# The up stage of a ConvFFN, last column: prompts copied out of their bank, a product moved whole, two moves at the front

## The chip, the core and the metric

The kernel runs on one core of a Trainium2 chip. The metric is the device time of one execution in microseconds (us), as the median of several runs.

A core has five engines, each with its own queue of instructions: TensorE (PE, the matmuls; PEld are its weight loads), VectorE (DVE), ScalarE (ACT), GpSimd (POOL) and SyncE (SP, which only issues transfers). They read and write the on-chip memory SBUF; matmuls write into PSUM, which has banks of 512 numbers of 32 bits in each of 128 partitions, and DVE and ACT read those. An engine waits on semaphores that another engine raises.

## The reference

One layer of a diffusion backbone for 1024 latent tokens (a grid of 16 rows of 64) and 128 context tokens ("prompts"), width 1024, everything in 32-bit floats. After a mixer comes the part that the change is in:

```python
def dw_conv(u, conv_w, conv_b, grid):   # grid: 3x3 depthwise; context: width 3
    ...
def conv_ffn(h, w_up, conv_w, conv_b, w_down, grid):
    u = dw_conv(h @ w_up, conv_w, conv_b, grid)
    gate, up = jnp.split(u, 2, axis=-1)
    return (jax.nn.silu(gate) * up) @ w_down
...
    x = x + gate2 * conv_ffn(h, w_ffn_up, ffn_conv, b_ffn_conv, w_ffn_down, grid)
```

The hidden width is 2 x 2816: `h @ w_up` has 5632 channels, half of them gates.

## The kernel before

**Precision.** A 32-bit product is made of three matmuls of a split: each operand x is a high part (`wuh`, `b11h`, ... copied with rounding by ACT, L1759 or L133) and a low part, x minus the high part (`wul`, `b11l`, ... one subtraction on POOL or DVE in `split_lo`, L69). So every product is (high, high), (high, low), (low, high) over four pieces of the contraction, 12 matmuls of 128x512.

**Up stage.** It makes `h @ w_up` for the grid's tokens in 22 columns c = 0 to 21 of 128 hidden channels, each with gates and ups. A column is done by a scheme of the Strassen kind with seven products (`up(c, p)`, L1976, L1777): 1 takes b11, 2 b21, 3 b22, 4 t4, 5 t1, 6 t2, 7 t3, where b and t are halves of the activations and their sums. They go into two accumulators of two banks each, `F = u[c][0]` (gates) and `S = u[c][1]` (ups); half of `S`, called X in the code, collects products 1, 6, 7 and 4. ACT copies X after product 1 (`cp`, by the name `p1`) and after product 6 (`u2p`, by the name `u2`), L1971, and DVE adds these copies to the others (L2134, L2135, L2160; in column 0 L1864, L1869, L1870 in `first_sums`). Product 6 cannot write X until `cp` has been copied, nor product 7 until `u2p` has. There are three accumulators for two that each column needs, so S of a column takes the banks of F of the column before, and F those of S two columns before.

**Convolution.** ACT writes the middle tap and the bias into `acc` (L1931), and DVE adds the eight other taps, each one `scalar_tensor_tensor` over the column (L1943, `acc <- u * weight + acc`, u in PSUM). The F convolution of a column runs before the S convolution (the second one, `second_half`). The last tap frees the accumulator. Then ACT takes the silu of the gates (L2043) and POOL multiplies gates by ups (L2045) and stores the result (L2046).

**Prompts.** The prompts of a column are 24 small matmuls (L2009); ACT copies them, PE transposes them (L2026) into a bank `x`, and `conv_prompt` does the width-3 convolution from there: one ACT instruction (L1956) and two DVE taps of 128x127 (L1960) for gates and the same for ups.

**Order.** PE's products go in the order of the loop at L2059: 5, (transposes and product 4 of the column before), 2, 3, 1, first prompt half, 6, second prompt half, 7. The last column differs: product 3 stands as six matmuls before product 1 and six behind, the prompts' halves go around product 7, and its product 4 has no next column to stand in. A scheduler orders the other engines' instructions by its own estimate of times, so a small edit can move rows far from it. POOL and DVE make the weights' low parts, POOL and SP issue the transfers.

**Down stage.** It begins behind the last column with product `xb` (L2279, 12 matmuls for each of 11 pairs of weights, `wuh`/`wul` or `wh`/`wl`), which goes into four banks; it takes the first three pairs through one bank after the other, then each further pair through all four. The third bank is that of the last column's transposed prompts. POOL makes the low parts of its first weight pairs, DVE those of pairs 7 to 10.

Of the kernel before, what the change touches and what calls it, by code (L numbers as in the profile page):

```python
# [12 lines left out]
AF = mybir.ActivationFunctionType  # L13
ALU = mybir.AluOpType
# [3 lines left out]
P = 128  # L18
# [6 lines left out]
NHID = 22  # L25
# [24 lines left out]
def kernel(ctx: ExitStack, tc: tile.TileContext, ins, outs, stop=None):  # L50
    nc = tc.nc
# [10 lines left out]
    anchor = {}  # L62
# [339 lines left out]
    for i in range(2):  # L402
# [3 lines left out]
        for v in range(2):  # L406
            dst = bass.AP(t.tensor, t.offset + v * pitch, [[32 * pitch, 2], [1, 512]])
# [4 lines left out]
    for i in range(2):  # L412
        ps = (ps_a, ps_mm)[i].tile([2 * 32, 512], F32, name="ada", tag=("ada", "mm")[i])
        psA.append(ps)
        for kt in range(KT):
# [4 lines left out]
            for j in range(2):  # L420
# [4 lines left out]
                    start=(kt == 0),  # L425
                    stop=(kt == KT - 1),
# [867 lines left out]
    def run(eng, fn):  # L1294

        if ran.get("free"):
            return fn()
        with tc.issue_after(ran[eng].ins) if eng in ran else nullcontext():
            ran[eng] = fn()
# [103 lines left out]
    tt = nc.vector.tensor_tensor  # L1403
# [7 lines left out]
    def half_hi(nm, n, raw):  # L1411
        run("act", lambda: nc.scalar.activation(HB["h"][nm][:, :, pieces[n]], raw, AF.Copy))
# [348 lines left out]
    def split_slots(c, names, eng):  # L1761
        hi, lo = split_parts(c, names)
        hi()
        return lo(eng)
# [5 lines left out]
        eng.tensor_tensor(r["s4"], r["12"], r["s2"], op=ALU.subtract)  # L1770
        return eng.tensor_tensor(r["s3"], r["11"], r["21"], op=ALU.subtract)

    def up_product(dst, c, a, b, start, stop, kts=range(4)):
        n = 3 * kts[0]
        for kt in kts:
            for x, y in (("h", "h"), ("h", "l"), ("l", "h")):
                last = mm(  # L1777
                    dst,
                    w_slot(c, a, x)[:, kt, :],
                    HB[y][b][:, kt, :],  # L1780
                    start=(start and n == 0),
                    stop=(stop and n == 11),
                    skip_group_check=True,
                )
                n += 1
        return last
# [71 lines left out]
    def first_sums():  # L1858

        F, S = u[0]  # L1860
        for n in range(2):
            token_sum(tmp[2 + n], rb(1, 0, n), tmp[2 + n])
        new_tiles("t4", 1)
        run("dve", lambda: tt(S[:, 512:NS], S[:, 0:512], copies["p5"], op=ALU.add))  # L1864
        half_hi("t4", 0, tmp[2])
        half_hi("t4", 1, tmp[3])
        for n in range(2):
            half_lo("t4", n, tmp[2 + n])
        run("dve", lambda: tt(F[:, 0:512], F[:, 0:512], copies["p1"], op=ALU.add))  # L1869
        run("dve", lambda: tt(F[:, 512:NS], F[:, 512:NS], copies["u2"], op=ALU.add))  # L1870
        second_lo("11", "12", eng="dve")

# [93 lines left out]
    def chained(fn):  # L1966

        run("pe", fn)
# [4 lines left out]
            return run("act", fn)  # L1973
        anchor["copy"] = fn()

    def up(c, p, kts=range(4)):  # L1976

        if p in (2, 3, 5):
            Z, Y = u[c][0][:, 0:512], u[c][0][:, 512:NS]
        else:  # L1980
            X = u[c][1][:, 0:512]
        chained(
            {
                1: lambda: up_product(X, c, "11", "b11", True, False),
                2: lambda: up_product(Z, c, "12", "b21", True, True),
                3: lambda: up_product(Y, c, "s4", "b22", False, True, kts),
                4: lambda: up_product(X, c, "22", "t4", False, True),
                5: lambda: up_product(Y, c, "s1", "t1", True, False),
                6: lambda: up_product(X, c, "s2", "t2", False, False),
                7: lambda: up_product(X, c, "s3", "t3", False, False),  # L1990
            }[p]
        )
        if p == 5 and c:
            copy(c, "p5", Y)
        elif p == 1:
            copy(c, "p1", X)
        elif p == 6:
            copy(c, "u2", X)
# [22 lines left out]
    def prompt_columns(c):  # L2021
        pp = ps_p.tile([P, 2, P], F32, name="x", tag="x")

        def turned():
            for i in range(2):
                last = nc.tensor.transpose(pp[:, i, :], pt_t[:, i * P : (i + 1) * P], ident)  # L2026
            return last

        chained(turned)
        up_first = SLOT[c]["21"] < SLOT[c]["11"]  # L2030
        with after("conv") if c < 2 else nullcontext():
            conv_prompt(pp[:, 1 if up_first else 0, :], c, acc[c][0])
            conv_prompt(pp[:, 0 if up_first else 1, :], 22 + c, acc[c][1])
# [25 lines left out]
    for c in range(NHID + 1):  # L2059
        n = c + 1 if c + 1 < NHID else None  # L2060
        if c < NHID:
            acc[c] = conv_tiles(c)
            u[c] = [ps_u.tile([P, NS], F32, name="u", tag="u")]

        if c == 0:
            u[0].append(ps_u.tile([P, NS], F32, name="u", tag="u"))
            for p in (1, 2):
                up(0, p)
        if c < NHID:
            up(c, 5)  # L2070
        if c == 0:
            prompt_work()
        if c == 1:
            for names in (("s2", "s4"), ("21", "22")):
                second_hi(*names)
                second_lo(*names)
            second_weights()
        if c == NHID:
            up(c - 1, 4)
            prompt_columns(c - 1)  # L2080
            second_half(c - 1)
        elif c > 0:
            prompt_columns(c - 1)
            up(c - 1, 4)
            second_half(c - 1)
        if c == NHID:
            break
        if c > 1 and n:
            split_slots(n, ("21", "22"), nc.gpsimd)
            if n + 1 < NHID:  # L2090
                load_row(n + 1, 2)
        last_c = c == NHID - 1
        if c > 0:
            up(c, 2)
            if not last_c:
                up(c, 3)
        pks[c] = ps_p.tile([P, 2 * P], F32, name="x", tag="x")
        if c == 1:
            up_prompt(c, 0)
            up_prompt(c, 1)  # L2100
        if c > 0:
            if last_c:
                up(c, 3, range(2))
            u[c].append(ps_u.tile([P, NS], F32, name="u", tag="u"))
            up(c, 1)
            if c == 1:
                anchor["p1"] = anchor["copy"]
                second_gate(0)
            if last_c:
                up(c, 3, range(2, 4))  # L2110
        if 1 < c and not last_c:
            up_prompt(c, 0)
        up(c, 6)
        if last_c:
            up_prompt(c, 0)
            up(c, 7)
        if c == 0:
            up(c, 3)
            up_prompt(c, 0)
            second_hi("s1")  # L2120
            second_lo("s1", eng="dve")
            second_hi("11", "12")
        if c and n:
            with tc.issue_after(anchor["p1"].ins) if c == 1 else nullcontext():
                split_slots(n, ("s1",), nc.gpsimd)
                split_slots(n, ("11", "12"), nc.gpsimd)
            if n + 1 < NHID:
                load_row(n + 1, 1)
        F, S = u[c]
        if c == 0:  # L2130
            up(c, 7)
            first_sums()
        else:
            nc.vector.tensor_tensor(F[:, 0:512], F[:, 0:512], copies["p1"], op=ALU.add)  # L2134
            nc.vector.tensor_tensor(F[:, 512:NS], F[:, 512:NS], copies["u2"], op=ALU.add)  # L2135
        if c != 1:
            up_prompt(c, 1)
        if c == 0:
            late = again["late"].tile([P, 2304], F32, name="late", tag="mh7")
            ss_t = late[:, 0:2048].rearrange("p (i n) -> p i n", i=4)  # L2140
            pt_t = late[:, 2048:2304]
        copy_pt = lambda: nc.scalar.activation(pt_t, pks[c], AF.Copy)
        if c == 0:
            run("act", copy_pt)
            with tc.issue_after(ran["act"].ins), tc.issue_after(ran["dve"].ins):
                anchor["conv"] = conv_rows(F, c, acc[c][0])
            ran["act"] = anchor["rows"]
        else:
            copy_pt()
        if c > 0 and n:  # L2150
            with tc.issue_after(anchor["copy"].ins) if c == 1 else nullcontext():
                split_slots(n, ("s2", "s4"), nc.gpsimd)
        if c == 1:
            with tc.issue_after(anchor["copy"].ins):
                split_slots(n, ("21", "22"), nc.gpsimd)
            load_row(n + 1, 2)
        if c > 0:
            if not last_c:
                up(c, 7)
            nc.vector.tensor_tensor(S[:, 512:NS], S[:, 0:512], copies["p5"], op=ALU.add)  # L2160
        if c > 0:
            anchor["conv"] = conv_rows(F, c, acc[c][0])
        if c > 0 and n:
            split_slots(n, ("s3",), nc.gpsimd)
            if n + 1 < NHID:
                weight_sums(n + 1, nc.gpsimd)
# [265 lines left out]
```

## Time and profile before

| | |
|---|---|
| runs | 1519.69, 1519.78, 1520.42 us; median 1519.78 |
| the profiled execution | 1517.37 us, its span 1515.2 us, mean granted clock of TensorE 0.996 |
| busy | PE 97%, DVE 76%, ACT 52%, POOL 47% of the span |
| PE's waits over 0.2 us from 785 us on, until the down stage has started | 785.18 (0.27), 797.88 (1.20), 801.58 (0.69), 806.01 (1.41), 809.49 (0.47), 834.18 (2.28), 1249.81 (1.28), 1271.72 (2.07) |

A row of a timeline reads: start in us, duration in us, engine, line of the kernel, operation, out<-in, shape, and how many instructions are joined in it (x2: the duration is that of both). In brackets is the time that the engine sat idle before it, and what it waited for. A row of the waits has the total in us, how many times, and the longest. A row of one line's instructions has min/median/max in ns. Column 1 of the up stage begins near 787 us, column 3 near 834; the last ends near 1265.

### The profile page before, as it was taken

The numbers are of one execution on the slowest core, as the hardware profiler recorded it, in microseconds if no ns is written. First come the engines' busy times: TensorE is split into PE (matmuls) and PEld (weight loads), VectorE is DVE, ScalarE is ACT, GpSimd is POOL, SyncE is SP. The second block draws the span as 40 slices with busy tenths as digits, with TensorE's granted clock in tenths as the row PEclk, the third lists the DMA queues.
The fourth block names the chain that finished last, engine by engine and source line by source line (L and its number), as shares of the span: only waits on it lengthen the run. The fifth ranks groups of instructions, "written<-read, shape, count | busy, mean of one in ns | idle before, by whom it ended". The sixth has DMA issues, their size and how long they took to land.

```text
span 1515.2 us, 31139 instructions
## 1 busy us (share of the span) xinstructions
PE 1464.7 (97%) x12509; PEld 1247.6 (82%) x12509; DVE 1145.1 (76%) x1735; ACT 781.1 (52%) x1519; POOL 705.0 (47%) x537
## 2 busy tenths in 40 slices
PE   6999999999999999899998999999999999999998
PEld 2898998999898988777776888888888877888886
DVE  3766566565565767755699999999999999689575
ACT  3575667555455455613765444444444444466444
POOL 1602122334333241222229999999999996100001
PEclk9999999999999999999999999999999999999999
DMA  9311111335535463967642745445644567989762
GB/s 341 134 44 48 45 57 52 117 98 171 162 97 184 120 203 121 334 247 251 219 142 89 244 115 144 119 119 139 196 119 139 169 154 215 371 267 368 241 191 115
DMA packets 173802, 253.79 MB, mean 167 GB/s; under 512 B 11828, under 2 KB 113698, under 8 KB 171738
## 3 DMA queue, kind: packets, MB, share of 16 engines
q1 hardware_dynamic: 150455, 173.52, 36.0%
q0 software_dynamic: 22592, 77.60, 16.6%
q8 instruction: 98, 1.61, 0.5%
q10 hardware_dynamic: 611, 0.68, 0.1%
q14 instruction: 46, 0.38, 0.1%
HBM read 191.93 MB, written 82.90 MB: 181 GB/s over the span
## 4 chain that ended last, share of the span: by engine, by line
PE 79%; DVE 7%; DMA 5%; ACT 3%; issue 3%; POOL 2%; SPq 0%; POOLq 0%; DVEq 0%; ACTq 0%
PE u L1777 24%; PE mm L625 15%; PE xb L2279 8%; PE yb L2279 6%; PE mm L639 5%; PE x L2009 4%; PE lv L964 3%; DVE acc L1943 3%; PE mm L777 2%; PE yb L2333 2%; PE u L1544 2%; PE x L1032 1%; PE mm L519 1%; DMA raw<-in_w_in_dram 1%; PE ada L1201 1%
## 5 line engine op out<-in xcount | busy, mean ns | idle before, releaser
L1943 DVE SCALAR_TENSOR_TENSOR acc<-u,convc,acc 128x945 f32<-128x945 f32 (+2 forms) x352 | 426.9, 1218 | 8.9 <-ACT acc L1931 1.8
L69 POOL TENSOR_TENSOR wl<-raw,wh 128x1024 fp32r<-128x1024 f32 x42 | 103.0, 2466 | 249.8 <-ACT wh L133 194.2
L625 PE MATMUL mm<-h1h,wh 128*128 128x384 f32 x528 | 185.0, 350 | 1.3 <-ACT qj L528 1.3
L625 PE MATMUL mm<-h1l,wh 128*128 128x384 f32 x528 | 179.0, 339 | 0.0
L625 PE MATMUL mm<-h1h,wl 128*128 128x384 f32 x528 | 179.0, 339 | 0.0
L927 DVE TENSOR_TENSOR Q<-Q,fb 128x384 f32<-128x384 f32 x126 | 81.9, 650 | 82.4 <-PE lv L964 81.4
L69 POOL TENSOR_TENSOR wul<-sr,wuh 128x512 fp32r<-128x512 f32 (+1 forms) x64 | 115.0, 1799 | 38.6 <-ACT wuh L1759 38.6
L69 POOL TENSOR_TENSOR wul<-ra,wuh 128x1024 fp32r<-128x1024 f32 x43 | 110.0, 2559 | 6.6 <-ACT wuh L133 6.5
L917 ACT ACTIVATE m<-k 128x384 f32<-128x384 f32 x126 | 70.2, 557 | 79.9 <-DVE k L929 37.2
L2243 POOL TENSOR_TENSOR sq<-sq,mhalf 128x1 f32<-128x1 f32 x9 | 11.1, 1231 | 205.8 <-DVE sq L2242 205.8
L625 PEld LDWEIGHTS mm<-h1h,wh 128*128 128x128 f32 x528 | 99.5, 188 | 6.2 <-issue 3.9
L625 PEld LDWEIGHTS mm<-h1l,wh 128*128 128x128 f32 x528 | 99.5, 188 | 0.6 <-issue 0.2
L625 PEld LDWEIGHTS mm<-h1h,wl 128*128 128x128 f32 x528 | 99.3, 188 | 0.8 <-issue 0.5
L639 PE MATMUL mm<-wh,h1h 128*128 128x256 f32 x288 | 83.8, 291 | 1.5 <-ACT v L664 1.5
L929 DVE TENSOR_TENSOR k<-k,fb 128x384 f32<-128x384 f32 x126 | 74.2, 589 | 12.3 <-ACT m L917 7.2
L639 PE MATMUL mm<-wh,h1l 128*128 128x256 f32 x288 | 80.4, 279 | 0.0
L639 PE MATMUL mm<-wl,h1h 128*128 128x256 f32 x288 | 80.4, 279 | 0.0
L133 ACT ACTIVATE wh<-raw 128x1024 fp32r<-128x1024 f32 x50 | 52.8, 1058 | 38.5 <-PE mm L625 11.6
L1971 ACT ACTIVATE u2p<-u 128x512 f32<-128x512 f32 x44 | 26.5, 602 | 77.3 <-PE u L1777 76.7
L1759 ACT ACTIVATE wuh<-ra 128x1024 fp32r<-128x1024 f32 x42 | 44.3, 1054 | 36.6 <-issue 22.1
L2045 POOL TENSOR_TENSOR acc<-acc,acc 128x1152 f32<-128x1152 f32 x22 | 60.0, 2730 | 5.0 <-DVE acc L1943 5.0
L1759 ACT ACTIVATE wuh<-sr 128x512 fp32r<-128x512 f32 (+1 forms) x63 | 48.7, 773 | 23.1 <-PE x L2009 16.4
(385 smaller groups left out, 4464.1 us busy)
## 6 DMA issues: line engine op xcount, KB each, us to landing
ra<-in_w_ffn_up_dram SPq DMA_DIRECT2D x84, 256.0 KB, 3.5
raw<-in_w_in_dram SPq DMA_DIRECT2D x32, 512.0 KB, 4.5
v<-in_w_ada_dram SPq DMA_DIRECT2D x27, 512.0 KB, 5.1
scr_g<-acc POOLq DMA_DIRECT2D x22, 576.0 KB, 5.6
scr_s<-late POOLq DMA_DIRECT2D x11, 1024.0 KB, 4.3
scr_t<-in_w_ffn_down_dram POOLq DMA_DIRECT2D x16, 704.0 KB, 7.3
wa<-in_w_ada_dram SPq DMA_DIRECT2D x16, 512.0 KB, 5.3
scr_t<-in_w_ffn_down_dram POOLq DMA_DIRECT2D x2, 2816.0 KB, 12.5
```

Of the source, the lines that this page charges most:

```text
L69: return eng.tensor_tensor(out, full, hi.bitcast(F32), op=ALU.subtract)
L625: anchor["fill"] = mm(ps, a[:, kt, :], h[kt][b], start=(n == 0), stop=(n == 23))
L639: anchor["fill"] = mm(ps, h[kt][t // 3][:, ts_], a[:, kt % 4, :], start=(n == 0), stop=(n == 23))
L917: nc.scalar.activation(aps(t, 0, [[2 * h, NB], [h, 2], [1, h]]), aps(src, 0, [[2 * h, NB], [BL + h, 2], [1, h]]), AF.Copy)
L927: nc.vector.tensor_tensor(qm, qm, aps(ff_, 2 * h - 1, [[BL - h, 2], [2 * h, NB], [0, h]]), op=ALU.mult)
L929: nc.vector.tensor_tensor(km, km, aps(ff_, BL + 2 * h - 1, [[-(BL + h), 2], [2 * h, NB], [0, h]]), op=ALU.mult)
L1759: return lambda: nc.scalar.activation(hi, raw, AF.Copy), lambda eng: split_lo(eng, lo, raw, hi)
L1777: last = mm(dst, w_slot(c, a, x)[:, kt, :], HB[y][b][:, kt, :], start=(start and n == 0), stop=(stop and n == 11), skip_group_check=True,)
L1943: last = nc.vector.scalar_tensor_tensor(o, u3[:, r0 + dy : r1 + dy, c0 + dx : c1 + dx], wc(3 * (dy + 1) + dx + 1), o, op0=ALU.mult, op1=AL ...
L2009: last = mm(pk, HB[h]["p"][:, 4 * half + kt, :], aps(flat(W[x]), a * 512 + kt * P, [[(b - a) * 512, 2], [1, P]]), start=(half + kt + n == ...
L2045: last = nc.gpsimd.tensor_tensor(accg, accg, accu, op=ALU.mult)
L2279: anchor["down"] = mm(banks[i][:, cs], w[a][:, ts_], w[b][:, 512 + cs.start : 512 + cs.stop], start=(start and j == 0 and n == 0), stop=(j ...
```

## The change

Four edits, in order of the diff. (1) `up_product` always does its 12 matmuls, so the last column's product 3 stands whole ahead of product 1. (2) In `first_sums`, the first add into F stands ahead of the two low parts of t4 on DVE. (3) In the last column ACT copies the bank of the transposed prompts, 128x256, into the SBUF tile of `cp`, and `conv_prompt` reads the copy, on ACT and on DVE. (4) In column 1 the splits of "11" and "12" for the next column are issued after the `u2p` copy.

```diff
-    def up_product(dst, c, a, b, start, stop, kts=range(4)):
-        n = 3 * kts[0]
-        for kt in kts:
+    def up_product(dst, c, a, b, start, stop):
+        n = 0
+        for kt in range(4):
...
         run("dve", lambda: tt(S[:, 512:NS], S[:, 0:512], copies["p5"], op=ALU.add))
+        run("dve", lambda: tt(F[:, 0:512], F[:, 0:512], copies["p1"], op=ALU.add))
         half_hi("t4", 0, tmp[2])
         half_hi("t4", 1, tmp[3])
         for n in range(2):
             half_lo("t4", n, tmp[2 + n])
-        run("dve", lambda: tt(F[:, 0:512], F[:, 0:512], copies["p1"], op=ALU.add))
...
         chained(turned)
+        if c == NHID - 1:
+            held = p1_t[:, 0 : 2 * P]
+            nc.scalar.activation(held, pp.rearrange("p i n -> p (i n)"), AF.Copy)
+            pp = held.rearrange("p (i n) -> p i n", i=2)
...
             up(c, 2)
-            if not last_c:
-                up(c, 3)
+            up(c, 3)
...
-            if last_c:
-                up(c, 3, range(2))
             u[c].append(ps_u.tile([P, NS], F32, name="u", tag="u"))
             up(c, 1)
...
-            if last_c:
-                up(c, 3, range(2, 4))
...
                 split_slots(n, ("s1",), nc.gpsimd)
+            with tc.issue_after(anchor["copy"].ins) if c == 1 else nullcontext():
                 split_slots(n, ("11", "12"), nc.gpsimd)
```

Below are three places where the order of instructions differs, as pieces of the difference: `-` stands in the program before, `+` in the changed one. Lines behind L2026 have numbers that are 4 higher in the changed kernel up to L2090.

On DVE, at the change from column 2 to column 3, `acc3` is the second convolution of column 1, `acc1` the first convolution of column 2, and `u_10665` and `u_10747` are F and S of column 2:

```order
 L1960 SCALAR_TENSOR_TENSOR acc3_10298<-x_10679,convc_8784,acc3_10298 128x127
+L1943 SCALAR_TENSOR_TENSOR acc3_10298<-u_10592,convc_8784,acc3_10298 128x16x63 x2
 L2134 TENSOR_TENSOR u_10665<-u_10665,cp1_10251 128x512
-L1943 SCALAR_TENSOR_TENSOR acc3_10298<-u_10592,convc_8784,acc3_10298 128x16x63 x2
+L1943 SCALAR_TENSOR_TENSOR acc3_10298<-u_10592,convc_8784,acc3_10298 128x15x63
+L1943 SCALAR_TENSOR_TENSOR acc3_10298<-u_10592,convc_8784,acc3_10298 128x960
 L2135 TENSOR_TENSOR u_10665<-u_10665,u2p5_10302 128x512
 L1943 SCALAR_TENSOR_TENSOR acc3_10298<-u_10592,convc_8784,acc3_10298 128x15x63
-L1943 SCALAR_TENSOR_TENSOR acc3_10298<-u_10592,convc_8784,acc3_10298 128x960
 L1943 SCALAR_TENSOR_TENSOR acc1_10297<-u_10665,convc_8784,acc1_10297 128x15x63
-L1943 SCALAR_TENSOR_TENSOR acc3_10298<-u_10592,convc_8784,acc3_10298 128x15x63
 L2160 TENSOR_TENSOR u_10747<-u_10747,u2p5_10302 128x512
```

Two taps of the second convolution have moved ahead of L2135, and its last tap ahead of the first tap of the next convolution.

On DVE in the last column, `acc1` takes its first convolution (gates), `acc0` its second (ups), `x_14041` is the bank of the transposed prompts and `cp1` the copy in SBUF:

```order
 L1943 SCALAR_TENSOR_TENSOR acc1_10297<-u_13880,convc_8784,acc1_10297 128x16x63
-L1960 SCALAR_TENSOR_TENSOR acc1_10297<-x_14041,convc_8784,acc1_10297 128x127
+L1960 SCALAR_TENSOR_TENSOR acc1_10297<-cp1_10251,convc_8784,acc1_10297 128x127
+L1960 SCALAR_TENSOR_TENSOR acc0_9782<-cp1_10251,convc_8784,acc0_9782 128x127
 L1943 SCALAR_TENSOR_TENSOR acc1_10297<-u_13880,convc_8784,acc1_10297 128x16x63
-L1960 SCALAR_TENSOR_TENSOR acc1_10297<-x_14041,convc_8784,acc1_10297 128x127
+L1960 SCALAR_TENSOR_TENSOR acc1_10297<-cp1_10251,convc_8784,acc1_10297 128x127
+L1960 SCALAR_TENSOR_TENSOR acc0_9782<-cp1_10251,convc_8784,acc0_9782 128x127
 L1943 SCALAR_TENSOR_TENSOR acc1_10297<-u_13880,convc_8784,acc1_10297 128x15x63
-L1960 SCALAR_TENSOR_TENSOR acc0_9782<-x_14041,convc_8784,acc0_9782 128x127
 L1943 SCALAR_TENSOR_TENSOR acc1_10297<-u_13880,convc_8784,acc1_10297 128x960
-L1960 SCALAR_TENSOR_TENSOR acc0_9782<-x_14041,convc_8784,acc0_9782 128x127
```

The four prompt taps stand in two pairs with one column tap between, and read `cp1` instead of `x`.

On POOL in the last column, L2045 (L2049 in the changed kernel) multiplies column 20's gates by its ups, `wul<-sr` in the last row is the low part of weight pair 3 of the down stage, and `wl0`, `wl1` are low parts of later pairs:

```order
 L69 TENSOR_TENSOR wul_10293<-ra_10290,wuh_10292 128x1024
 L69 TENSOR_TENSOR wul_10293<-sr_10291,wuh_10292 128x1024
-L2045 TENSOR_TENSOR acc3_10298<-acc3_10298,acc2_9783 128x1152
+L69 TENSOR_TENSOR wl0_14092<-raw0_14097,wh0_14091 128x1024
+L2049 TENSOR_TENSOR acc3_10298<-acc3_10298,acc2_9783 128x1152
 L1916 DMA scr_t3_157<-in_w_ffn_down_dram 32x11x512
-L69 TENSOR_TENSOR wl0_14091<-raw0_14096,wh0_14090 128x1024
-L69 TENSOR_TENSOR wl1_14093<-raw1_14097,wh1_14092 128x1024
+L69 TENSOR_TENSOR wl1_14094<-raw1_14098,wh1_14093 128x1024
 L69 TENSOR_TENSOR wul_10293<-sr_10291,wuh_10292 128x1024
```

One low part has moved ahead of the gate product and the transfer; the rest keeps its order.

More of the change, by code (lines that the diff above doesn't have):

```diff
@@ L1974, in copy, with up @@
         anchor["copy"] = fn()
-    def up(c, p, kts=range(4)):
+    def up(c, p):
         if p in (2, 3, 5):
@@ L1985, in up @@
                 2: lambda: up_product(Z, c, "12", "b21", True, True),
-                3: lambda: up_product(Y, c, "s4", "b22", False, True, kts),
+                3: lambda: up_product(Y, c, "s4", "b22", False, True),
                 4: lambda: up_product(X, c, "22", "t4", False, True),
```

## The prediction

> **What bounds the kernel now.** I read the page's busy times first, then a table of stretches of the up stage, then the list of waits, then the timelines around each wait of TensorE (PE).
>
> ```profile
> PE 1464.7 (97%) x12509; PEld 1247.6 (82%) x12509; DVE 1145.1 (76%) x1735; ACT 781.1 (52%) x1519; POOL 705.0 (47%) x537
> ...
> 835.00:1245.00 410.00, 410.00 (x2008) 340.04 (x2007) 397.57 (x420) 190.23 (x255) 394.62 (x264) 1.00 0.54 151
> ...
> PE u L1777 <- DVE acc L1943: 5.2, 4, 2.3
> PE xb L2279 <- DVE acc L1960: 2.1, 1, 2.1
> ```
>
> The second row is the stretch 835 to 1245 us, with the busy time of PE, of its weight loads, of VectorE (DVE), ScalarE (ACT) and GpSimd (POOL). PE is busy 97% of the span, and in this stretch, columns 3 to 20, all 410.00 of 410. So the change can win only at the two ends of the up stage, where four waits on convolution taps (L1943, 5.2 us), one on a prompt tap (L1960, 2.1) and waits on copies (L1971) stand. DVE with 397.57 and POOL with 394.62 of 410 have little room. The waits at the front:
>
> ```profile
> 797.88 0.50 PE L1777 MATMUL u<-b11h,wuh 128*128 128x512 f32 x1 [1.20 <-DVE acc L1943]
> 806.01 0.50 PE L1777 MATMUL u<-t3h,wuh 128*128 128x512 f32 x1 [1.41 <-ACT u2p L1971]
> 809.49 0.47 PE L1777 MATMUL u<-t1h,wuh 128*128 128x512 f32 x1 [0.47 <-DVE acc L1943]
> 831.29 0.39 PE L1777 MATMUL u<-t3l,wuh 128*128 128x512 f32 x1
> 831.51 0.39 PE L1777 MATMUL u<-t3h,wul 128*128 128x512 f32 x1
> 834.18 0.47 PE L1777 MATMUL u<-t1h,wuh 128*128 128x512 f32 x1 [2.28 <-DVE acc L1943]
> ```
>
> **The front (columns 1 to 3).** On DVE and ScalarE (ACT) stand:
>
> ```profile
> 782.76 2.36 DVE L69 TENSOR_TENSOR t4l<-acc,t4h 128x1024 fp32r<-128x1024 f32 x2 [0.52 <-ACT t4h L1412]
> 785.04 0.69 DVE L1869 TENSOR_TENSOR u<-u,cp 128x512 f32<-128x512 f32 x1
> ...
> 804.44 1.04 ACT L1759 ACTIVATE wuh<-ra 128x1024 fp32r<-128x1024 f32 x1
> 805.38 0.57 ACT L1971 ACTIVATE u2p<-u 128x512 f32<-128x512 f32 x1
> ...
> 828.41 0.70 DVE L2135 TENSOR_TENSOR u<-u,u2p 128x512 f32<-128x512 f32 x1 [0.99 <-ACT u2p L1971]
> 829.02 2.45 DVE L1943 SCALAR_TENSOR_TENSOR acc<-u,convc,acc 128x945 f32<-128x945 f32 x2
> 831.73 2.31 DVE L1943 SCALAR_TENSOR_TENSOR acc<-u,convc,acc 128x945 f32<-128x945 f32 x2 [0.26 <-ACT acc L1931]
> ```
>
> The add of L1869 takes 0.69 and moves into the idle 0.52 ahead of 782.76: the first convolution starts 0.7 earlier, the t4l parts 0.1 later at most. PE's b11 of column 1 gains the 0.7. The u2p copy no longer stands behind wuh<-ra (805.38 - 804.44 = 0.94), so t3 starts 1.4 earlier in all; wuh<-ra, displaced by the copy's 0.5, is for the next column and nobody waits. But t1 of column 2 waits for the last tap of column 0's second convolution, and the new order puts L2160 (0.6) ahead of that tap: it still ends near 809.4, and PE is back where it was (0 to +0.1). What has moved is DVE's whole stream.
>
> At 834.18 it pays. Before, DVE idles 0.99 for u2p, does two taps, waits 0.26 for ACT, does a tap of the next convolution and then the tap that PE waits for. In the new order two taps stand ahead of L2135, in the idle time, and the awaited tap stands ahead of the one that waits for ACT: it ends about 829.1 + 1.2 to 830.7, while PE gets there at 831.51 + 0.23 = 831.74. The start-to-start gap of 2.67 shrinks to a step of 0.23 (831.51 - 831.29 = 0.22): 2.44, less 0.1 for the late t1 and 0.1 to 0.2 for rounding: **-2.2**. Ends: -2.44, and 0 if DVE cannot follow in the columns after (below).
>
> **The last column, PE and ACT.**
>
> ```profile
> 1249.81 0.50 PE L1777 MATMUL u<-b11h,wuh 128*128 128x512 f32 x1 [1.28 <-DVE acc L1943]
> 1254.03 0.39 PE L1777 MATMUL u<-t2h,wuh 128*128 128x512 f32 x1
> ...
> 1252.87 0.60 ACT L1971 ACTIVATE cp<-u 128x512 f32<-128x512 f32 x1 [1.85 <-PE u L1777]
> 1263.27 0.38 ACT L2142 ACTIVATE late<-x 128x256 f32<-128x256 f32 x1
> ...
> 1271.72 0.47 PE L2279 MATMUL xb<-wuh 128*128 128x512 f32 x1 [2.07 <-DVE acc L1960]
> 1276.15 0.39 PE L2279 MATMUL xb<-wul,wuh 128*128 128x512 f32 x1
> ```
>
> Six b22 matmuls (six steps of 0.22 to 0.23, 1.36) move ahead of b11 and fill its wait, but they had stood between b11 and t2, and hid the cp copy (L1971): that copy ends at 1253.47, so t2 starts at about 1253.5 instead of 1254.03: **-0.5** (ends 0 and -1.4).
>
> The copy of the prompts' bank is one ACTIVATE more; the nearest row, late<-x of the same 128x256, takes 0.38, in a queue with idle time around it. It frees the bank near 1267, before PE wants it (1271.72 - 2.07 = 1269.65), so the 2.07 goes. Next late is POOL:
>
> ```profile
> 1259.53 3.27 POOL L69 TENSOR_TENSOR wul<-ra,wuh 128x1024 fp32r<-128x1024 f32 x1 [6.53 <-ACT wuh L133]
> 1265.14 2.68 POOL L2045 TENSOR_TENSOR acc<-acc,acc 128x1152 f32<-128x1152 f32 x1
> 1267.76 1.08 POOL L1916 DMA_DIRECT2D scr_t<-in_w_ffn_down_dram  x1
> 1268.48 5.10 POOL L69 TENSOR_TENSOR wl<-raw,wh 128x1024 fp32r<-128x1024 f32 x2
> 1273.16 2.79 POOL L69 TENSOR_TENSOR wul<-sr,wuh 128x1024 fp32r<-128x1024 f32 x1
> ```
>
> The last row is the low half of weight pair 3, done at 1275.95, used at 1276.15. POOL's rows only change order and start 0.5 to 0.9 sooner (with ACT's copies, which wait for t2, and a shorter overlap at the first row, 3.27 where a split alone takes 2.4), so PE waits 1.7 here, and of 2.07 + 0.5 only **-0.9** remains. If nothing else happened the sum would be -2.2 - 0.9 = -3.1, -2.7 with less from POOL.
>
> **The last column, the four prompt taps.** They read the copy, so both their large inputs, cp and acc, lie in SBUF. Before, x lay in PSUM. The trace prices both kinds and shows DVE and POOL take turns:
>
> ```profile
> 1267.06 0.34 DVE L1960 SCALAR_TENSOR_TENSOR acc<-x,convc,acc 128x127 f32<-128x127 f32 x1
> ...
> L1960 DVE SCALAR_TENSOR_TENSOR acc<-x,convc,acc x88: 339/342/353, 797.7 to 1271.2; 128x127 f32<-128x127 f32 x88
> L1049 DVE SCALAR_TENSOR_TENSOR st<-st,tl x42: 335/351/2375, 198.0 to 692.0; 128x128 f32<-128x128 f32 x42
> ...
> 526.25 2.36 POOL L69 TENSOR_TENSOR wl<-raw,wh 128x1024 fp32r<-128x1024 f32 x1 [4.28 <-ACT wh L133]
> 525.99 3.15 DVE L1049 SCALAR_TENSOR_TENSOR st<-st,tl 128x128 f32<-128x128 f32 x3
> ...
> 1282.53 1.22 DVE L69 TENSOR_TENSOR wul<-ra,wuh 128x1024 fp32r<-128x1024 f32 x1
> 1283.66 5.93 DVE L69 TENSOR_TENSOR wul<-sr,wuh 128x1024 fp32r<-128x1024 f32 x2
> 1289.52 2.31 DVE L69 TENSOR_TENSOR wul<-raw,wuh 128x1024 fp32r<-128x1024 f32 x1
> 1282.76 3.52 POOL L2045 TENSOR_TENSOR acc<-acc,acc 128x1152 f32<-128x1152 f32 x1 [4.95 <-DVE acc L1943]
> 1288.60 2.15 POOL L1897 TENSOR_TENSOR late<-late,acc 128x512 f32<-128x512 f32 x1
> ```
>
> No tap from PSUM was ever stretched (353 ns at most, 88 of them, beside a POOL that was busy 394.62 of 410). The same operation and size with two SBUF inputs took up to 2375 ns: one that meets a POOL operation stands until that ends. From 1282.53 on the two engines go in turn: L2045 takes 3.52 instead of 2.68 behind wul<-ra, the next DVE split waits it out, and the one after that takes 2.31 instead of 1.22 beside L1897.
>
> The Trainium skill, page "SBUF — State Buffer", section "Who interferes with whom", has this as a rule that speaks against the change: VectorE with two SBUF inputs and GpSimd reading SBUF share an exclusive lock, held for a whole instruction, and an operation with one SBUF input is outside it. By that rule the four taps are blocked; the trace agrees with both halves (2375 and 353 ns). Priced by the old L1960 row instead (4 x 0.34), nothing is blocked and the sum stays -2.7 to -3.1.
>
> I lay the new POOL order end to end on the old clock, front gain left out and with 2.36 for a split: wul<-ra from 1259.0 (1259.53 less the 0.5) to 1262.0, wul<-sr to 1264.35, wl<-raw to 1266.7, L2045 to 1269.35, the DMA to 1270.0 (1268.48 - 1267.76 = 0.7), wl<-raw to 1272.4, wul<-sr. DVE, late by 0.3 (below), comes to its first prompt tap at 1267.3, before at 1267.06: it stands 2.0 behind L2045. The second follows in the DMA's gap, free. A PSUM tap (1.2), then the third at 1271.0 stands 1.4 behind wl<-raw. POOL's wul<-sr, waiting by then, goes next, and the fourth stands 2.35 behind it. Together **5.8**; ends 0, and 8.2 if the second meets a POOL operation too.
>
> Who pays: behind the taps on DVE are the other taps, then the low halves of weight pairs 7 and 8.
>
> ```profile
> 1287.03 0.39 PE L2279 MATMUL xb<-wul,wuh 128*128 128x512 f32 x1
> 1289.75 0.39 PE L2279 MATMUL xb<-wul,wuh 128*128 128x512 f32 x1
> ```
>
> Pair 7's is done at 1283.75 and used at 1287.03: slack 3.3. Pair 8's is done at 1282.76 + 3.52 + 1.1 = 1287.4 and used at 1289.75: slack 2.35, 2.2 with the hand-over. DVE enters the last column 2.2 early and loses 0.3 to 0.4 waiting for cp, since L2134 now stands a tap earlier: -1.8. So PE ends -1.8 + 5.8 - 2.2 = +1.8, with 0.1 for restarting: **+1.9**. PE's own gains (-3.1 until here) are swallowed by waits at pairs 7 (about 4) and 8 (about 1). After that the trace shows PE without slack to win it back.
>
> The profiled run took 1517.37 (span 1515.2); the median of the three others is 1519.78, 2.41 more. 1517.37 + 1.9 = 1519.3 in the profile's terms, **1521.7** as median. About 0.2% (3.04 us) is what a measurement of this kernel tells from no change, so this is within it.
>
> **Rivals.** With B for the blocked time and G for the front gain kept, PE ends at about B - G + 0.4 - 2.2 + 0.1, and at best at -3.1.
>
> 1. Slower: the front gain does not last. DVE follows a PE that is 2.2 earlier only out of its idle time, 410 - 397.57 = 12.4 over 18 columns, 0.7 in each. If a tap ends later than PE's b11 in columns 3 or 4, PE waits there and G falls to 0 to 1: +3.1 to +4.1, say +3.6: 1523.4. It decides from G below 1.1. For it: DVE's tight stream. Against: DVE's stream is itself 0.7 earlier, and waits for PE's sums.
> 2. Slower, by all four taps blocked: B = 8.2, +4.3: 1524.1. Against: the 0.65 DMA gap behind L2045 is wide enough for a 0.25 tap.
> 3. The fourth tap gets in ahead of wul<-sr: B = 3.4, -0.5: 1519.3. Against: the turns from 1282.53 on.
> 4. The copy does as meant, no blocking: -2.7 to -3.1, 1516.9. For it: L1960's 88 rows. Against: L1049's 2375.
>
> **Chances.** Forecast 0.49 (own range 1520.4 to 1523.2), rival 1 0.30, rival 2 0.05, rival 3 0.07, rival 4 0.09. Slower by over 0.2%: 0.10 of the forecast's, 0.25 of rival 1, all of 2: 0.40. Faster by over 0.2%: half of rival 4: 0.05. Within: 0.55. The range 1518.5 to 1524.5 leaves out rival 4 and the outer ends.
>
> **What would show it.** Right: the wait at t1 of column 3 gone; L1960 with a maximum above 2 us; PE waits at xb on DVE's wul of 4 and 1 us, and at pair 3 on POOL. Wrong: four L1960 rows near 0.3 (rival 4), or PE waits on L1943 in columns 3 to 20 (rival 1).

## The result, and the profile after

The changed kernel takes 1526.14 us (median of five runs, 1525.46 to 1529.91; before in the same comparison 1519.69): ratio 1.0045, 95% interval 1.0031 to 1.0058. It is slower by more than the 0.2% that can be told from no change, and outside the predicted range. The profiled execution took 1525.46 (span 1523.0), before 1517.37 (span 1515.2): the span is 7.8 longer. Below, PE's lateness is the start of a TensorE matmul less the start of the same matmul of before. It stands at 1.57 already at 779 us, ahead of every edit, and that is a difference from run to run: in the profiles of the runs below it lies between -1.4 and +2.8 at this place. 6.2 came behind it.

The page's busy times of the kernel after, and the same stretch of columns 3 to 20:

```profile
PE 1468.0 (96%) x12509; PEld 1250.1 (82%) x12509; DVE 1153.3 (76%) x1735; ACT 780.5 (51%) x1520; POOL 704.1 (46%) x537
...
835.00:1245.00 410.00, 409.95 (x2005) 339.61 (x2004) 398.59 (x420) 189.90 (x255) 396.18 (x264) 1.00 0.54 151
```

PE is as full in the columns as before (409.95 of 410): no wait stands there. DVE is busy for 8.2 us more in all, with the same 1735 instructions: some of them stood. The two forms of the prompt tap, from the view of line L1960:

```profile
L1960 DVE SCALAR_TENSOR_TENSOR acc<-x,convc,acc x84: 339/343/351, 798.6 to 1249.5; 128x127 f32<-128x127 f32 x84
L1960 DVE SCALAR_TENSOR_TENSOR acc<-cp,convc,acc x4: 340/1268/6167, 1268.6 to 1278.2; 128x127 f32<-128x127 f32 x4
```

The 84 taps that still read the bank take 0.34 each; the four that read the copy together take 0.34 + 2 x 1.27 + 6.17 = 9.04 us (of four, the median is the mean of the middle two), 7.7 more than 4 x 0.34. Where they stood is seen by laying DVE's timeline beside POOL's:

```profile
1268.60 8.16 DVE L1960 SCALAR_TENSOR_TENSOR acc<-cp,convc,acc 128x127 f32<-128x127 f32 x2
1276.68 1.25 DVE L1943 SCALAR_TENSOR_TENSOR acc<-u,convc,acc 128x1008 f32<-128x1008 f32 x1
1277.86 0.73 DVE L1960 SCALAR_TENSOR_TENSOR acc<-cp,convc,acc 128x127 f32<-128x127 f32 x2
1278.51 13.61 DVE L1943 SCALAR_TENSOR_TENSOR acc<-u,convc,acc 128x945 f32<-128x945 f32 x11
1292.04 1.21 DVE L69 TENSOR_TENSOR wul<-ra,wuh 128x1024 fp32r<-128x1024 f32 x1
1293.17 3.67 DVE L69 TENSOR_TENSOR wul<-sr,wuh 128x1024 fp32r<-128x1024 f32 x1
```

```profile
1267.86 2.66 POOL L2049 TENSOR_TENSOR acc<-acc,acc 128x1152 f32<-128x1152 f32 x1
1270.47 1.10 POOL L1916 DMA_DIRECT2D scr_t<-in_w_ffn_down_dram  x1
1271.19 2.81 POOL L69 TENSOR_TENSOR wl<-raw,wh 128x1024 fp32r<-128x1024 f32 x1
1273.54 2.77 POOL L69 TENSOR_TENSOR wul<-sr,wuh 128x1024 fp32r<-128x1024 f32 x1
1275.85 0.99 POOL L2050 DMA_DIRECT2D scr_g<-acc  x1
1276.48 1.69 POOL L1898 TENSOR_TENSOR late<-acc 128x512 f32<-128x512 f32 x1
```

The first tap stands behind the gate product L2049 until 1270.5 (2.07). The second (6.17) starts there and does not end before 1276.7: it stands through the transfer (L1916) and both splits (L69). Between the splits DVE gets no turn. The third still meets the last 0.3 us of POOL's L1898 (1276.48 + 1.69 = 1278.17) and takes 0.46; the fourth finds POOL idle and takes 0.34. DVE comes to pair 7's low half (`wul<-ra`) at 1292.04, which ends 9.5 later than before's 1283.75.

PE's waits and its timeline:

```profile
PE xb L2279 <- DVE wul L69: 5.8, 1, 5.8
PE u L1777 <- DVE acc L1943: 2.9, 2, 2.0
PE xb L2279 <- POOL wul L69: 1.6, 1, 1.6
```

```profile
811.12 0.47 PE L1777 MATMUL u<-t1h,wuh 128*128 128x512 f32 x1 [1.98 <-DVE acc L1943]
812.06 0.63 PE L1777 MATMUL u<-t1h,wuh 128*128 128x512 f32 x1
812.49 0.63 PE L1777 MATMUL u<-t1l,wuh 128*128 128x512 f32 x1
834.99 0.39 PE L1777 MATMUL u<-t1h,wuh 128*128 128x512 f32 x1
1254.77 0.50 PE L1777 MATMUL u<-t2h,wuh 128*128 128x512 f32 x1 [0.69 <-ACT cp L1971]
1270.26 0.39 PE L2279 MATMUL xb<-wuh 128*128 128x512 f32 x1
1276.36 0.50 PE L2279 MATMUL xb<-wul,wuh 128*128 128x512 f32 x1 [1.63 <-POOL wul L69]
1293.31 0.80 PE L2279 MATMUL xb<-wul,wuh 128*128 128x512 f32 x1 [5.77 <-DVE wul L69]
1293.90 0.63 PE L2279 MATMUL xb<-wuh,wul 128*128 128x512 f32 x1
1294.33 0.63 PE L2279 MATMUL xb<-wuh 128*128 128x512 f32 x1
```

The waits at t1 of column 3 and at the bank (2.28 and 2.07 before) are gone, as the rows at 834.99 and 1270.26 show; at pair 3 stands 1.63 on POOL, at pair 7 5.77 on DVE. One thing more: behind 812.06 and 1293.90 a matmul takes a step of 0.43 instead of 0.23. The view of stretches shows why:

```profile
813.00:815.00 2.00, 2.00 (x6) 1.59 (x5) 1.93 (x3) 0.00 (x0) 2.00 (x2) 0.50 0.03 8
1293.00:1295.00 2.00, 1.69 (x4) 1.40 (x5) 2.00 (x2) 0.00 (x0) 2.00 (x1) 0.50 0.30 73
```

The seventh number behind the window is TensorE's granted clock: 0.50 in both. PE's lateness grows by 1.6 behind t1 of column 2 and by 1.5 behind pair 7, as if it had waited that much longer.

So PE's lateness goes +1.57 (run to run, 779), +0.80 (t1 of column 3, with the first 1.6 of half clock in it), +1.21 (ahead of b11 of the last column), +0.21 (pair 3), +6.28 (pair 7), +7.80 (behind the half clock), and stays.

### The profile page after: what moved, and what is told of

It is laid out like the page before. It is cut to its first block, busy times and chain, and to the rows that moved or that the text cites. A ratio compares the mean times of both kernels' runs of the same rounds, so it can differ in the third digit from the quotient of the medians.

```text
span 1523.0 us, 31143 instructions
## 1 busy us (share of the span) xinstructions
PE 1468.0 (96%) x12509; PEld 1250.1 (82%) x12509; DVE 1153.3 (76%) x1735; ACT 780.5 (51%) x1520; POOL 704.1 (46%) x537
## 4 chain that ended last, share of the span: by engine, by line
PE 74%; DVE 6%; DMA 6%; POOL 5%; issue 5%; ACT 3%; SPq 0%; POOLq 0%; DVEq 0%; ACTq 0%
PE u L1777 20%; PE mm L625 15%; PE xb L2279 7%; PE yb L2279 6%; PE mm L639 5%; PE mm L777 3%; PE x L2009 3%; PE lv L964 3%; DVE acc L1943 2%; PE yb L2333 2%; POOL wul L69 2%; PE u L1544 2%; PE x L1032 2%; PE mm L519 1%; DMA raw<-in_w_in_dram 1%
## 5 line engine op out<-in xcount | busy, mean ns | idle before, releaser
L1943 DVE SCALAR_TENSOR_TENSOR acc<-u,convc,acc 128x945 f32<-128x945 f32 (+2 forms) x352 | 426.9, 1218 | 8.8 <-ACT acc L1931 1.7
L69 POOL TENSOR_TENSOR wl<-raw,wh 128x1024 fp32r<-128x1024 f32 x42 | 102.8, 2449 | 249.9 <-ACT wh L133 192.1
L69 POOL TENSOR_TENSOR wul<-sr,wuh 128x512 fp32r<-128x512 f32 (+1 forms) x64 | 115.9, 1810 | 37.3 <-ACT wuh L1759 37.2
L69 POOL TENSOR_TENSOR wul<-ra,wuh 128x1024 fp32r<-128x1024 f32 x43 | 109.9, 2555 | 6.6 <-ACT wuh L133 6.1
L2049 POOL TENSOR_TENSOR acc<-acc,acc 128x1152 f32<-128x1152 f32 x22 | 60.1, 2730 | 14.1 <-DVE acc L1943 14.1
L2047 ACT ACTIVATE acc<-acc 128x1152 f32<-128x1152 f32 x22 | 25.7, 1170 | 70.9 <-DVE acc L1943 70.9
```

The lines of the kernel that those rows point to most:

```text
L69: return eng.tensor_tensor(out, full, hi.bitcast(F32), op=ALU.subtract)
L1943: last = nc.vector.scalar_tensor_tensor(o, u3[:, r0 + dy : r1 + dy, c0 + dx : c1 + dx], wc(3 * (dy + 1) + dx + 1), o, op0=ALU.mult, op1=AL ...
L2049: last = nc.gpsimd.tensor_tensor(accg, accg, accu, op=ALU.mult)
```

## The experiments

The theory is that the four prompt taps, through their second SBUF input, stand behind POOL, and that this alone turns a gain of 2 to 3 us into the loss. The rivals: the loss comes from one of the other edits, or from the order that they make together; or the half clock is the cause. All ratios are against the kernel before, on the same chip; they are not the quotients of the two medians, from which they differ by up to 0.001.

**The change without the copy.**

```diff
-        if c == NHID - 1:
-            held = p1_t[:, 0 : 2 * P]
-            nc.scalar.activation(held, pp.rearrange("p i n -> p (i n)"), AF.Copy)
-            pp = held.rearrange("p (i n) -> p i n", i=2)
```

> The changed kernel without the copy of the prompts' bank: the taps read PSUM again. Theory A (the loss is the four taps, blocked by POOL 7.9 us in all, and a half TensorE clock after the long wait that follows): DVE's four taps take 0.34 each, PE's wait of 5.8 on DVE's low half is gone, and the kernel is 1 to 3 us faster than before (front gain 0.8 if the clock drops after t1 of column 2 as in the changed kernel, 2.4 if it does not, and 0.5 to 0.9 in the last column). Theory B (the loss is in the reordered rows of the front and of the last column, the taps only move a wait): still 3 us or more slower than before.

Measured: 1517.12, before 1519.67, ratio 0.9990 (0.9978 to 1.0002); profiled 1514.37. Four L1960 taps of the last column are back at 0.34, PE has no wait at pair 7, and the bank's wait is back:

```profile
1268.78 0.47 PE L2275 MATMUL xb<-wuh 128*128 128x512 f32 x1 [2.09 <-DVE acc L1960]
```

The other three edits cost nothing that the runs can tell; the copy costs about 8 us with them around it (1517.12 to 1525 or 1526).

**The copy alone**, those four lines in the kernel before.

> The kernel before with the copy of the prompts' bank as the only edit. Theory A: DVE's taps stand for 6 to 8 us in all behind POOL's low halves, PE waits 4 to 6 us for DVE's low half of pair 7, and loses 1.3 more to a half clock behind that wait: 4 to 7 us slower than before. Theory B: the 2.07 wait at the bank turns into a wait for POOL's low half of pair 3, 0 to 1 us faster.

Measured: 1527.0, ratio 1.0053 (1.0039 to 1.0067). L1960, DVE's and POOL's timelines, and PE's two waits:

```profile
L1960 DVE SCALAR_TENSOR_TENSOR acc<-cp,convc,acc x4: 334/1041/7339, 1269.9 to 1281.4; 128x127 f32<-128x127 f32 x4
...
1271.55 8.84 DVE L1960 SCALAR_TENSOR_TENSOR acc<-cp,convc,acc 128x127 f32<-128x127 f32 x2
1270.24 1.07 POOL L1916 DMA_DIRECT2D scr_t<-in_w_ffn_down_dram  x1
1270.96 5.12 POOL L69 TENSOR_TENSOR wl<-raw,wh 128x1024 fp32r<-128x1024 f32 x2
1275.67 2.71 POOL L69 TENSOR_TENSOR wul<-sr,wuh 128x1024 fp32r<-128x1024 f32 x1
...
1278.43 0.50 PE L2283 MATMUL xb<-wul,wuh 128*128 128x512 f32 x1 [2.01 <-POOL wul L69]
1295.24 0.50 PE L2283 MATMUL xb<-wul,wuh 128*128 128x512 f32 x1 [4.01 <-DVE wul L69]
```

The copy by itself makes the whole loss. One tap of 0.25 to 0.34 us stood 7.34 us, through three splits in a row, and again the stretch begins behind the transfer L1916. This tap comes only when the transfer's row has ended (1270.24 + 1.07 = 1271.31, the tap near 1271.55), and still gets no turn between the splits. With 0.33 + 2 x 1.04 + 7.34 - 1.36, 8.4 us were blocked. Both waits were followed by a spell of half clock, of some 1.7 us each; by the medians the loss is 7.3, a little more than the 4 to 7 expected.

**The front alone** (edits 2 and 4) and **the whole product alone** (edit 1):

```diff
 e3: front
+        run("dve", lambda: tt(F[:, 0:512], F[:, 0:512], copies["p1"], op=ALU.add))
...
-        run("dve", lambda: tt(F[:, 0:512], F[:, 0:512], copies["p1"], op=ALU.add))
...
+            with tc.issue_after(anchor["copy"].ins) if c == 1 else nullcontext():
                 split_slots(n, ("11", "12"), nc.gpsimd)
 e4: product
-            if not last_c:
-                up(c, 3)
+            up(c, 3)
...
-            if last_c:
-                up(c, 3, range(2))
...
-            if last_c:
-                up(c, 3, range(2, 4))
```

> The kernel before with only the two edits at the front (the first sum's add ahead of t4's low halves, the splits of 11 and 12 behind the u2p copy). Theory A: the wait of 2.28 at t1 of column 3 is gone, a wait near 2.0 stands at t1 of column 2; 2.4 us faster where the clock stays full behind it, 0.8 faster where it halves for 3.4 us. Theory B: 1 us or more slower than before.

> The kernel before with only the whole product 3 ahead of product 1 in the last column. Theory A: b11's wait of 1.28 becomes a wait of 0.7 for the cp copy at t2 (0.5 gained), the prompt taps come a column tap earlier and the bank's wait of 2.07 shrinks by some tenths: 0.3 to 1.0 us faster. Theory B: the reordered rows on POOL and DVE make it 1 us or more slower.

Measured: the front 1517.2, ratio 0.9993 (0.9982 to 1.0004); the product 1518.46, ratio 0.9999 (0.9988 to 1.0011). Neither can be told from no change by its time. In their traces:

```profile
809.38 0.47 PE L1777 MATMUL u<-t1h,wuh 128*128 128x512 f32 x1 [1.98 <-DVE acc L1943]
```

```profile
1254.21 0.50 PE L1777 MATMUL u<-t2h,wuh 128*128 128x512 f32 x1 [0.69 <-ACT cp L1971]
1271.96 0.47 PE L2274 MATMUL xb<-wuh 128*128 128x512 f32 x1 [2.09 <-DVE acc L1960]
```

The front takes away the wait at t1 of column 3 and wins 2.4 us against the same matmuls of before (their difference goes from -0.18 to -2.57). Columns 3 to 20 take 0.5 of it back in small steps (-2.06 at the last b22), and behind the bank's wait, 2.10 here, this profile has a spell of half clock that takes 1.6 more. The product moved whole wins 0.4 at t2 (0.70 to 0.32), since PE now waits for `cp` (0.69) instead of doing matmuls; the bank's wait then stands at 2.09, as long as before, where it was expected to shrink by some tenths.

**The four taps later.** They read the copy, so nobody waits for them until ACT's silu ahead of the last gate product; here they are issued behind the fifth tap of the last convolution, where POOL is idle.

```diff
...
+                conv_prompt(*args, sides=c < NHID - 1)
+        if c == NHID - 1:
+            held_taps.append(lambda: [conv_prompt(*args, mid=False) for args in both])
...
+        if held_taps:
+            with tc.issue_after(row_taps[-4].ins):
+                held_taps.pop()()
```

> The changed kernel with the copy kept, but DVE's four prompt taps issued behind the fifth tap of the last convolution, when POOL has no work. Theory A (blocked by POOL, not the copy or the second SBUF operand as such): the four taps take 0.33 to 0.35 each, the bank's wait of 2.07 stays gone, PE waits about 1.6 for POOL's low half of pair 3, and no longer for DVE's of pair 7: 2.5 to 3.5 us faster than the kernel before, 8 to 10 faster than the changed one. Rival C (two SBUF inputs make a tap slow by themselves, or the copy holds up ACT): the taps stay above 1 us each or the kernel is no faster than before.

Measured: 1516.26, before 1518.76, ratio 0.9978 (0.9969 to 0.9986): faster. DVE's rows of the four taps, and PE's one wait in the down stage's first pairs:

```profile
1275.06 0.60 DVE L1964 SCALAR_TENSOR_TENSOR acc<-cp,convc,acc 128x127 f32<-128x127 f32 x2
1276.69 0.61 DVE L1964 SCALAR_TENSOR_TENSOR acc<-cp,convc,acc 128x127 f32<-128x127 f32 x2
...
1271.61 0.50 PE L2291 MATMUL xb<-wul,wuh 128*128 128x512 f32 x1 [1.66 <-POOL wul L69]
```

The same instruction with the same two SBUF inputs takes 0.34 where no such POOL operation runs. So it is neither the copy nor its place in SBUF that costs, but what runs beside it. By the ratios (1.0045 and 1.0039 below, against 0.9978) moving the taps is worth 9 to 10 us to the changed kernel.

**The same, with POOL's low half of pair 3 ahead of those of pairs 4 and 5**, against the wait of 1.66.

```diff
...
-            split_lo(eng, lo, raw, hi)
+            with tc.issue_after(los[behind].ins) if behind in los else nullcontext():
+                los[key] = split_lo(eng, lo, raw, hi)
...
+        return load_w([a, b], [2 * 512], nc.gpsimd if p == 1 and j < 6 else nc.vector, (p, j), (1, 3) if p == 1 and j in (4, 5) else None)
```

> As the one with the late taps, and POOL makes the low half of weight pair 3, which PE needs first, ahead of those of pairs 4 and 5. Theory A: the wait of 1.6 at pair 3 goes as well, a few tenths may come back at pair 8: 1 to 1.6 us faster than the one with late taps alone, 4 to 5 faster than before. Rival: the low halves of pairs 4 and 5 are then late and give it back.

Measured: 1515.5, ratio 0.9973 (0.9963 to 0.9982). The wait at pair 3 is gone, and 0.60 remains at pair 8, on DVE. By their ratios this and the late taps alone can't be told apart. The waits tell the chain: behind the bank POOL's order is next, and behind that DVE's low halves.

**The change without POOL's transfer L1916** between the gate product and the splits; its work is left to the next call.

```diff
-        if sums_todo and c > 0:
+        if sums_todo and c > 0 and c != NHID - 2:
```

> The changed kernel with the one transfer that POOL issues behind the last but one gate product left to the next column, so that POOL's gate product and its three low halves stand back to back. Theory A1 (POOL keeps the port from one operation to the next as long as it has one ready): DVE's first tap itself stands until the last low half is done, one row of 6.5 to 8 us, the others 0.3 to 0.5. Theory A2 (the two engines take turns, as I forecast): four rows of 2 to 2.5 us each. Theory A3 (the transfer was what blocked the second tap): first tap about 2 us, second at most 2.7. Time: within 1.5 us of the changed kernel for A1 and A2, 2 to 4 us faster than it for A3.

Measured: 1523.07, ratio 1.0032 (1.0021 to 1.0042). The four taps, and DVE beside POOL:

```profile
L1960 DVE SCALAR_TENSOR_TENSOR acc<-cp,convc,acc x4: 1302/2016/2483, 1266.5 to 1273.3; 128x127 f32<-128x127 f32 x4
...
1266.50 4.49 DVE L1960 SCALAR_TENSOR_TENSOR acc<-cp,convc,acc 128x127 f32<-128x127 f32 x2
1272.09 3.17 DVE L1960 SCALAR_TENSOR_TENSOR acc<-cp,convc,acc 128x127 f32<-128x127 f32 x2
1265.75 2.69 POOL L2049 TENSOR_TENSOR acc<-acc,acc 128x1152 f32<-128x1152 f32 x1
1268.39 2.45 POOL L69 TENSOR_TENSOR wl<-raw,wh 128x1024 fp32r<-128x1024 f32 x1
1270.80 2.44 POOL L69 TENSOR_TENSOR wul<-sr,wuh 128x1024 fp32r<-128x1024 f32 x1
```

Now the engines do go in turn: one tap passes between two POOL operations, and each tap stands about one of them. In the changed kernel, where POOL's rows behind the transfer overlap (1271.19 + 2.81 = 1274.00 is behind 1273.54, where here 1268.39 + 2.45 = 1270.84 is 0.04 behind 1270.80), no tap passes between. So it is the transfer at this place that takes DVE's turns away. A transfer of POOL's doesn't do so everywhere. In the kernel before, these two rows stand ahead of L1897:

```profile
1286.57 0.58 POOL L2046 DMA_DIRECT2D scr_g<-acc  x1 [0.30 <-POOL acc L2045]
1287.17 1.35 POOL L1896 TENSOR_TENSOR late<-acc,acc 128x512 f32<-128x512 f32 x1
```

Behind the transfer L2046 POOL's rows don't overlap (1287.17 + 1.35 = 1288.52, and L1897 starts at 1288.60), and DVE's splits and POOL's operations go in turn there. What the places without a turn have in common is the overlap. Nor is the transfer the cause of the loss: without it 1.30 + 2 x 2.02 + 2.48 - 1.36 = 6.5 us are blocked instead of 7.7, and PE still waits 5.52 at pair 7.

**The best version**: the late taps and pair 3 as above, and L2160 of column 1 issued behind the awaited tap, against the wait of 1.98 that the front edit leaves at t1 of column 2. Beside it **the changed kernel again**.

```diff
-            nc.vector.tensor_tensor(S[:, 512:NS], S[:, 0:512], copies["p5"], op=ALU.add)
+            with tc.issue_after(row_taps[-1].ins) if c == 1 else nullcontext():
+                nc.vector.tensor_tensor(S[:, 512:NS], S[:, 0:512], copies["p5"], op=ALU.add)
```

> The late taps and pair 3 first, and in column 1 the sum L2160 behind the last tap of column 0's second convolution, for which t1 of column 2 waits. Theory A: that wait shrinks from 1.98 to about 1.4, the rest stays: 4 to 5 us faster than before, 0.4 to 0.6 faster than without this edit, which the runs can hardly tell. Rival: DVE's stream is the bound in the columns after, and nothing or a new wait comes of it.

> The changed kernel once more, on the same chip as the best version. Theory A: the first prompt taps stand 8 us in two rows as before, the wait at pair 7 is 5 to 6, and a half clock behind it costs 1.5 to 2.5 again; whether a half clock follows the wait of 1.98 at t1 of column 2 differs from run to run, so that the runs scatter by 1.6. 4.5 to 7 us slower than before. Rival: the half clock at t1 of column 2 belongs to the change and comes back in each profile, 6.5 or more slower.

Measured: the best version 1513.84, before 1519.52, ratio 0.9966 (0.9953 to 0.9978); the changed kernel again 1524.82, ratio 1.0039 (1.0024 to 1.0053). By its ratio the best version can't be told from the one ahead of it (0.9973). It leaves these waits:

```profile
809.40 0.47 PE L1780 MATMUL u<-t1h,wuh 128*128 128x512 f32 x1 [1.40 <-DVE acc L1946]
1285.89 0.50 PE L2295 MATMUL xb<-wul,wuh 128*128 128x512 f32 x1 [0.62 <-DVE wul L69]
```

All four edits stay in it: the copy, which makes the loss, does free the bank, and seems to help once its taps stand clear of POOL (0.9990 without it, 0.9978 with it and the taps late; the two intervals overlap, and in the profiles the span, less the lateness at 779, is 0.5 shorter with it). The changed kernel's second profile has the same waits (1.66 at pair 3, 5.78 at pair 7), but no half clock behind t1 of column 2:

```profile
811.00:817.00 6.00, 4.65 (x21) 3.85 (x22) 5.89 (x6) 1.70 (x4) 6.00 (x4) 1.00 0.35 103
1292.86 0.80 PE L2279 MATMUL xb<-wul,wuh 128*128 128x512 f32 x1 [5.78 <-DVE wul L69]
1297.27 0.39 PE L2279 MATMUL xb<-wul,wuh 128*128 128x512 f32 x1
```

So that spell of 1.6 us is luck of the run: of the seven profiles with the wait of 1.98, only the first of the changed kernel and the one without the transfer have a spell behind it. The one behind pair 7 is there again (pair 7's twelve matmuls take 1297.27 - 1292.86 = 4.41 us, where before they take 1289.75 - 1287.03 = 2.72). In this profile PE is +2.80 late at 779, ahead of the edits, +0.45 behind the front and +7.51 at the end: the edits cost 4.7 us here and 6.2 in the first profile. The two medians say 5.3 and 6.5, but their intervals overlap.

## Why the prediction was wrong

The mechanism was named and priced, and the direction of the sum was right; the forecast of +1.9 was 3.4 to 4.6 us too small (+5.3 and +6.5 by the medians), and the time came out above the range. Point by point, the second profile of the changed kernel being the undisturbed one:

- **The front, -2.2.** Right: -2.35 (+2.80 to +0.45), and -2.4 alone; columns 3 to 20 take back 0.3 and 0.5, so that 1.9 to 2.0 is kept. That the wait at t1 of column 2 would leave PE "back where it was" was right too: it grew to 1.98, by the gain ahead of it. What was overlooked is that so long a wait can bring half a clock behind it, 1.6 us in the first profile.
- **Rival 1** (the front's gain doesn't last, 0.30) is refuted: 409.95 of 410, no L1943 wait in columns 3 to 20, and 1.9 to 2.0 kept where the rival needed less than 1.1. It had the largest chance on the slow side, and it was the wrong way to be slow.
- **The last column's product and bank, -0.9 together.** Right: from the last matmul ahead of b11 to pair 3, PE goes from +1.21 to +0.21, -1.0, with a wait of 1.63 on POOL where 1.7 was forecast. Alone the product wins 0.4 (forecast 0.5).
- **The four taps, 5.8.** This is the step that failed. That they are blocked was right, and the first tap's 2.0 too (2.07). "The second follows in the DMA's gap, free" was wrong: it took 6.17. POOL's transfer was no gap for the waiting tap, and behind it the two engines did not go in turn. By then both splits were done, so the third and fourth took 0.46 and 0.34 instead of standing 1.4 and 2.35. Measured 7.7, near rival 2's 8.2 though by another way; that rival had 0.05, on the strength of the gap, and its 1524.1 was the nearest of the five times. The evidence for turns (from 1282.53 on) was of a place where POOL's rows don't overlap, though a transfer (L2046) stands in it too; the prediction's own rows behind L1916 do overlap (1268.48 + 5.10 = 1273.58 is behind 1273.16). The run without the transfer shows turns indeed: the rule was read from a place that didn't have what this place has.
- **Who pays.** Right in kind: pair 7's low half came 9.5 late in the first profile, of which 7.7 is the blocked time, and PE waited 5.77 there where about 4 was forecast; the taps' 1.9 more than forecast is the difference.
- **The missing term.** Half the clock behind the wait at pair 7: 4.41 - 2.72 = 1.7 us. It hid the wait of about 1 forecast at pair 8 (in the second profile pair 8's low half comes at about 1296.4, and PE at full clock would have been there at 1292.86 + 2.72 = 1295.58), so about 0.8 of it is lost on top.
- **The sum**: +1.9, and 1.9 more of blocking, and 0.8 of clock, gives +4.6, where the second profile has +4.7 and the first, with its spell of 1.6 at the front, +6.2. No run takes the half clock away by itself; its share is read from these rows.

By the Trainium skill, page "SBUF — State Buffer", section "Who interferes with whom", the shared ports are an exclusive lock, and a VectorE instruction with two SBUF inputs contends with a GpSimd instruction that reads SBUF. The runs agree (0.34 from the bank or beside an idle POOL, up to 2.48 behind one POOL instruction). That a waiting instruction can stand through several of POOL's, as with 6.17 and 7.34, the page doesn't say; only these rows do.

## What to carry to other kernels

Before a VectorE operation is given a second SBUF input, look at what POOL does in that stretch, and place it where POOL is idle: the same four taps cost 7.7 us beside its splits and nothing 6 us later. Price such blocking, as its upper end, not by one POOL operation but by POOL's whole run of work up to its next real pause, above all where POOL's rows overlap behind a transfer. A wait of several microseconds on TensorE cost more than its length in all four profiles that had one: add the matmuls behind it at half clock (1.5 to 2.5 us here), then see which later wait that hides.

## What the runs showed of the hardware

- **A short VectorE operation can stand through several POOL operations.** One tap of 0.34 stood 6.17 us behind a transfer and two splits, 7.34 us behind three splits following a transfer; without the transfer, 2.48 at most. Behind the transfer POOL's rows overlap by some 0.45 us; behind another transfer in the kernel before (1286.57) they don't, and there the engines go in turn. Why the transfer L1916 takes the turns away stays open; it is only seen that it does.
- **Half the clock after short waits.** From 800 us on, waits of TensorE of 4.0 to 5.8 us were followed by a spell at granted clock 0.50 in each of the four profiles that had one (1.5 to 2.5 us lost). A spell lasts 3.4 or 6.8 us and can begin inside the wait, as in the first profile of the changed kernel (1289.53 to 1296.36, where PE goes on at 1293.31); what is lost is half of PE's busy time in it (3.05 us there, 1.5 lost). Waits of 1.98 to 2.28 us were followed by one in 6 of 15 cases: 1.98 at t1 of column 2 in 2 of 7 profiles, 2.28 at t1 of column 3 in 2 of 3, about 2.1 at the bank in 1 of 4, and 2.01 at pair 3 in the one with the copy alone. The Trainium skill, page "TensorE: Matmul & The Clock Gate", Part 1, gives about 3.4 us of idleness, one free-running window, as what to avoid. The long waits agree; the 1.98 shows that less can do, and that its coming is a matter of the run. That spell accounts for the 1.6 us between the two profiles of the changed kernel.
